# Mamba-2's z projected for two groups at once (512 columns, four PSUM banks) in groups 2 to 7

## The chip, the cores and the metric

One core of one Trainium2 chip runs the whole kernel in one launch. The metric is the device time of that launch in microseconds (us). The engines are named as in the profile: PE is the matrix engine (its weight loads are PEld), ACT the scalar engine, DVE the vector engine, POOL the general engine, SP the engine that issues DMAs.

## The reference, cut to what matters

Two layers over 512 tokens of width 1024, each a token mixer and a gated convolution. The first mixer is HGRN2, the second Mamba-2. The change is in Mamba-2, which has 8 groups of 4 heads:

```
def mamba2_mixer(u, w_in, ..., norm_w, w_out):
    z, xbc, dt_raw = jnp.split(u @ w_in, [D_INNER, D_INNER + CONV_DIM], axis=-1)
    xbc = jax.nn.silu(dwconv_centred(xbc, conv_w, conv_b))
    xs, bm, cm = jnp.split(xbc, [D_INNER, D_INNER + GN], axis=-1)
...
    y = (ssd_chunked(xs, dt_fw, a[0], bm, cm)
         + flip(ssd_chunked(flip(xs), flip(dt_bw), a[1], flip(bm), flip(cm)))
         + xs * d_skip.reshape(SSM_GROUPS, SSM_HPG, 1))
    y = y.reshape(bsz, seq, D_INNER) * jax.nn.silu(z)
    y = group_rmsnorm(y, norm_w, SSM_GROUPS)
    return y @ w_out
```

So z is a projection of u (512 tokens x 1024) to 2048 columns, 256 for each group. It is needed late in a group, where the group's y is multiplied by silu(z).

## The kernel before, in words

All projections are made of pairs of float32r values: every operand is split into a high and a low part, and a product is three matmuls (`mm3`, lines 164 to 166: high x high, low x high or high x low, and the other). A weight comes from HBM in pieces of 128 x 1024 floats through three `raw` buffers. ACT makes the high part of a piece (`whi`, line 138) and DVE the low one (`wlo`, line 139), four buffers each. The list `plan` fixes the order of the pieces, and `fetch` keeps two pieces ahead of the one in use.

Most projections hold a weight block still and stream u, 512 columns for a matmul (`proj_chs`). Only z (in Mamba) and one projection of HGRN2 are wanted with tokens on partitions: `proj_tok` holds a block of 128 tokens of u still and streams the 256 weight columns of one group. For z of one group that is 4 token blocks x 8 slices of the width x 3 = 96 matmuls of 256 columns, into two PSUM banks with two token blocks each.

PSUM has eight banks. `proj_ps` hands out three (`pp`), for projections and output projections, and `misc_ps` five (`pm`), for everything else. A bank is handed out again when the last instruction that reads it is done.

PE's order is written by hand. The string `MAMBA` (line 39) gives the order of the projections: `p` a group's B, C and x, `z` its z, `o` so many quarters of the output projection. `fill` issues them. Their length is counted in units, two units for six matmuls of 512 columns or for twelve of 256. The function `mix(g)` is the rest of group g, a generator whose nine steps are put into PE's stream at the units `STEPS` (33, 44, 45, 53, 56, 60, 64, 70, 89) after the start of the group's `p`, plus `LATE`. The order of ACT and DVE is not written by hand: the framework's scheduler decides it. The steps of `mix` that matter here, by their lines before:

- at 33: B is transposed into one `pm` bank (926) and B times C goes into another (931). ACT copies both out (927, 933).
- at 44: x is transposed into two `pm` banks (942), each copied out by ACT into `x_t` (943).
- at 53 and 56: the states of the two directions. Each takes two banks, `pa` with two products and `pb` with one (982). ACT copies the first product out (986), DVE makes the other two states by a multiply and an add each (991, 993), and only the adds read the bank.
- at 60 and 64: what the states give to the output, two banks each (1015), each read by one DVE multiply (1020).
- at 70: the products within a chunk into two banks (1030); DVE adds them and multiplies by silu(z) (1036, 1037). ACT squares, POOL makes the norm, ACT scales (1040 to 1045).
- at 89: y is transposed into two banks (1053). ACT writes its high part (`yh`, 1055) and DVE its low part (`yl`, 1056) from these banks. There are six `yh` and six `yl` buffers, so three groups' worth.

The output projection `out_part` takes groups in pairs: its quarters 0 to 3 read y of groups 0 and 1, 4 to 7 that of groups 2 and 3, 8 to 11 that of 4 and 5, and 12 to 15 that of group 6. A group's `yh` and `yl` buffers come free when the last quarter of its pair is done. Group 7 follows by itself.

Of the kernel before, what the change touches and what calls it, by code (L numbers as in the profile page):

```python
# [10 lines left out]
F32 = mybir.dt.float32  # L11
F32R = mybir.dt.float32r
I32 = mybir.dt.int32
U8 = mybir.dt.uint8
AF = mybir.ActivationFunctionType
# [4 lines left out]
P = 128  # L20
# [4 lines left out]
ND = D // P  # L25
# [10 lines left out]
LEVELS = (0, 5, 18, 32, 45)  # L36
ENDS = ((50, 55, 61, 67), (56, 61, 67, 74))

MAMBA = [(c[0], int(c[1:])) for c in "p0 z0 p1 z1 p2 z2 o1 p3 o1 z3 o2 p4 z4 o2 p5 z5 o2 p6 z6 p7 z7 o8".split()]

STEPS = (33, 44, 45, 53, 56, 60, 64, 70, 89)
LATE = {0: 21, 1: 1, 2: 4, 3: 4, 4: 2, 5: 3, 6: 3}
DTCOL = 64
SZ = 3

ARTANH = (0.11619523831039165, 0.1085165786592581, 0.14296291676788242, 0.19999850679099573, 0.33333333668798704)

# [12 lines left out]
def tile_trunk(ctx: ExitStack, tc: tile.TileContext, x, norm1_w, norm2_w, a_w_in, a_lb_logits, a_norm_w, a_w_out,  # L60
# [3 lines left out]
    V, A, G, PE = nc.vector, nc.scalar, nc.gpsimd, nc.tensor  # L64

    cst = ctx.enter_context(tc.tile_pool(name="cst", bufs=1))
    wp = ctx.enter_context(tc.tile_pool(name="wp", bufs=2))
    ps = ctx.enter_context(tc.tile_pool(name="ps", bufs=3, space=PSUM))
    dram = ctx.enter_context(tc.tile_pool(name="dram", bufs=1, space=DRAM))

    def proj_ps():
        return ps.tile([P, T], F32, tag="pp", name="pp", bufs=3)

    def misc_ps():
        return ps.tile([P, T], F32, tag="pm", name="pm", bufs=5)
# [12 lines left out]
    uhi = [cst.tile([P, T], F32R, name=f"uhi{d}") for d in range(ND)]  # L88
    ulo = [cst.tile([P, T], F32R, name=f"ulo{d}") for d in range(ND)]
    rbc = cst.tile([P, T], F32, name="rbc")  # L90
    ssum = cst.tile([P, T], F32, name="ssum")
    rtok = cst.tile([P, NB], F32, name="rtok")
# [20 lines left out]
    plan, ready = deque(), deque()  # L113

    def want(key, parts, nk):

        for k0 in range(0, nk, 4):
            plan.append((key, [x[k0 * P:min(nk, k0 + 4) * P] for x in parts]))

    def want_out(key, w_out, k0, nk):  # L120
        for c in range(4):
            want((key, c), [w_out[k0 * P:(k0 + nk) * P, c * 256:(c + 1) * 256]], nk)

    def load(parts):
        nk = parts[0].shape[0] // P
        raw = wp.tile([P, 4, 256], F32, tag="raw", name="raw", bufs=3)
        c0 = 0
        for src in parts:
            n = src.shape[1]
            nc.sync.dma_start(raw[:, :nk, c0:c0 + n], src.rearrange("(k p) c -> p k c", p=P))  # L130
            c0 += n
        return raw, nk, c0

    def halves(raw, nk, c0):
        hi = wp.tile([P, 4, 256], F32R, tag="whi", name="whi", bufs=4)
        lo = wp.tile([P, 4, 256], F32R, tag="wlo", name="wlo", bufs=4)
        r = raw[:, :nk, :c0]
        A.copy(hi[:, :nk, :c0], r)  # L138
        V.tensor_tensor(lo[:, :nk, :c0], r, hi[:, :nk, :c0].bitcast(F32), ALU.subtract)  # L139
        return hi, lo  # L140

    def fetch(n):
        while plan and len(ready) < n:
            k, parts = plan.popleft()
            ready.append((k, halves(*load(parts))))

    def take(key, ahead=2):

        got = []
        while (ready or plan) and (ready[0][0] if ready else plan[0][0]) == key:  # L150
            if not ready:
                k, parts = plan.popleft()
                ready.append((k, halves(*load(parts))))
            got.append(ready.popleft()[1])
        assert got, key
        fetch(ahead)

        def part(i, k, c0, n=P):
            return got[k // 4][i][:, k % 4, c0:c0 + n]

        return part

    def mm3(dst, lhi, llo, rhi, rlo, start, stop):
        PE.matmul(dst, lhi, rhi, start=start, stop=False)  # L164
        PE.matmul(dst, lhi, rlo, start=False, stop=False)  # L165
        PE.matmul(dst, llo, rhi, start=False, stop=stop)  # L166


    def proj_ch(p, w, c0):

        yield from proj_chs([(p, w, c0)])

    def proj_chs(ps):

        for k in range(ND):
            for p, w, c0 in ps:
                mm3(p, w(0, k, c0), w(1, k, c0), uhi[k], ulo[k], k == 0, k == ND - 1)
            if k % 2:
                yield 2 * len(ps)
# [97 lines left out]
    w_in = a_w_in[0]  # L277
# [16 lines left out]
    w_in = b_w_in[0]  # L294
    nout = 0
    for step in MAMBA:
        g = step[1]
        if step[0] == "p":
            want(("bc", g), [w_in[:, 4096 + P * g:4096 + P * (g + 1)], w_in[:, 5120 + P * g:5120 + P * (g + 1)]], ND)
            if g == 0:  # L300
                want("dt", [w_in[:, 6144:6208]] * 2, ND)
            want(("x", g), [w_in[:, 2048 + 256 * g:2048 + 256 * (g + 1)]], ND)
        elif step[0] == "z":
            want(("z", g), [w_in[:, 256 * g:256 * (g + 1)]], ND)
        else:
            for n in range(g):
                k, c = min(nout // 4 * 2, 6), nout % 4
                k1 = min(k + 2, 7)
                want((("bo", k), c), [b_w_out[0][2 * k * P:2 * k1 * P, c * 256:(c + 1) * 256]], 2 * (k1 - k))
                nout += 1  # L310
# [20 lines left out]
    parts = [plan.popleft()[1] for _ in range(4)]  # L331
# [94 lines left out]
    with tc.manual_schedule(engines={mybir.EngineType.PE, mybir.EngineType.DVE, mybir.EngineType.Activation}):  # L426
# [8 lines left out]
        w = halves(*raws[0])  # L435
# [12 lines left out]
        w = halves(*raws[2])  # L448
# [4 lines left out]
        w = halves(*raws[1])  # L453
# [4 lines left out]
        w = halves(*raws[3])  # L458
# [15 lines left out]
        w = take(("a", 0, 2))  # L474
# [305 lines left out]
    def mamba():  # L780
# [6 lines left out]
        def t2k(tag, bufs):  # L787
            return pool.tile([P, T], F32, tag=tag, name=tag, bufs=bufs)
# [25 lines left out]
        def r128(tag, bufs=2):  # L814
            return t2k(tag, bufs)[:, 0:H]

        def steps(x1):

            bias, na = dtbias, nega
            e, s, s2, acc = r128("sz", SZ), r128("th", 1), r128("pr"), r128("E1")  # L820
            V.tensor_scalar(x1, x1, bias, None, ALU.add)
# [42 lines left out]
            A.activation(fl(dec_t), fl(dec_t), AF.Exp)  # L864
            A.activation(fl(al_b), fl(al_b), AF.Exp)

        groups = {}

        def proj_group(g):
            wbc = take(("bc", g))  # L870
            r = []
            pbc, bc = [], ((16 + g, "sb", 1), (24 + g, "sc", 2))
            for i in range(2):
                pbc.append(proj_ps())
                if g == 0 and i == 0:
                    pd = proj_ps()
                    wd = take("dt")
                    yield from proj_chs([(pbc[0], wbc, 0), (pd, wd, 0)])
                else:
                    yield from proj_ch(pbc[i], wbc, i * P)  # L880
                if g > 0:
                    r.append(conv(pbc[i], i, *bc[i]))
            if g == 0:

                r.append(conv(pbc[0], 0, *bc[0]))
                x1 = r128("cb", 1)
                for n in range(2):
                    rs = slice(n * NR, (n + 1) * NR)
                    hs = slice(n * H, (n + 1) * H)
                    V.tensor_tensor(x1[rs], pd[rs, hs], rbc[rs, hs], ALU.mult)  # L890
                r.append(conv(pbc[1], 1, *bc[1]))
            wx = take(("x", g))
            for i in range(2):
                p = proj_ps()
                yield from proj_ch(p, wx, i * P)
                r.append(conv(p, i, 2 * g + i, "sx", 2))
                if g == 0 and i == 0:
                    step0 = steps(x1)
                    next(step0)
                    groups["steps"] = step0  # L900
            z = []
            groups[g] = (*r, z)

        def proj_z(g):
            z = groups[g][4]
            wz = take(("z", g))
            for c in range(2):
                p = proj_ps()
                yield from proj_tok(p, wz, (2 * c, 2 * c + 1))
                z.append(t2k("sz", SZ))  # L910
                for b in range(2):
                    bs = slice(b * 256, (b + 1) * 256)
                    A.activation(z[c][:, bs], p[:, bs], AF.Silu, scale=rtok[:, 2 * c + b:2 * c + b + 1])  # L913

        def h4(ap):

            return ap.rearrange("p n (h e) -> p n h e", e=64)
# [156 lines left out]
        def fill():  # L1074
            done = 0
            for kind, g in MAMBA:
                if kind == "p":
                    yield from proj_group(g)
                elif kind == "z":
                    yield from proj_z(g)  # L1080
                else:
                    done += g
                    while out_at[0] < out_units(done):
                        c = next(out_work)
                        out_at[0] += c
                        yield c
            yield from out_work

        def out_units(n):
            return 8 * min(n, 12) + 4 * max(n - 12, 0)  # L1090
# [8 lines left out]
        jobs, t, nout = [(scales(pool), [12, 18]), (step_columns(), [DTCOL])], 0, 0  # L1099
        for kind, g in MAMBA:  # L1100
            if kind == "p":
                if g == 0:
                    t += 8
                jobs.append((mix(g), [t + LATE.get(g, 0) + o for o in STEPS]))
                t += 32
            elif kind == "z":
                t += 16
            else:
                t += out_units(nout + g) - out_units(nout)
                nout += g  # L1110
# [112 lines left out]
```

## Time and profile before

| what | value |
|---|---|
| median of 3 runs | 1526.4 us (1526.35 to 1526.6) |
| time of the profiled execution | 1525.6 us |
| span of its instructions | 1523.8 us |
| PE busy | 1513.8 us, 99% of the span |
| DVE busy | 1040.2 us, 68% |
| ACT busy | 793.6 us, 52% |
| mean granted clock of PE | 0.999 |

The span is the time from the first to the last instruction. A launch is 1.8 us longer than it in the profiled execution. PE's busy time is the union of its matmuls, whose shown durations overlap their neighbours, so how long PE needs for a matmul is read from the distance of two starts, not from a duration.

### The profile page before, as it was taken

The page shows a single profiled execution, that of the slowest core. Times are in us where ns is not written, and L with a number is a line of the kernel's source. Part 1 is how long each engine was busy: PE and PEld are TensorE (multiplying, and loading weights), DVE is VectorE, ACT ScalarE, POOL GpSimd, SP SyncE. Part 2 cuts the span into 40 slices and gives each one's busy share as a digit, 9 for nine tenths or more (in the row PEclk, how much of TensorE's full clock was granted, in tenths as well). Part 3 has the DMA queues.
Part 4 walks back from the last instruction along what each step waited for, and adds up shares of the span by engine and source line. Part 5 has one row for each costly group of instructions (what it writes and reads, how often), then busy time and mean ns, then how long its engine had stood idle before and what let it go on. Part 6 is the DMA issues. An engine that isn't in the chain of part 4 may idle for free.

```text
span 1523.8 us, 24654 instructions
## 1 busy us (share of the span) xinstructions
PE 1513.8 (99%) x9935; PEld 1285.2 (84%) x9935; DVE 1040.2 (68%) x1695; ACT 793.6 (52%) x1427; POOL 29.3 (2%) x34
## 2 busy tenths in 40 slices
PE   9999999999999999999999999999999999999998
PEld 7888888888888888888888888888888888888887
DVE  6887786858564256545899978788878664346543
ACT  5656565545332133334699878569835433223333
POOL 0000000000000000000000000000000000000000
PEclk9999999999999999999999999999999999999999
DMA  5322222223333323223444343334223232323222
GB/s 186 111 76 67 70 72 64 70 77 111 97 97 97 97 97 98 90 90 109 129 138 138 124 124 116 108 114 128 66 79 122 86 110 84 97 97 111 76 83 77
DMA packets 153640, 151.65 MB, mean 100 GB/s; under 512 B 8390, under 2 KB 144279, under 8 KB 153527
## 3 DMA queue, kind: packets, MB, share of 16 engines
q1 hardware_dynamic: 153415, 149.93, 31.7%
q8 instruction: 78, 1.28, 0.4%
q14 instruction: 35, 0.29, 0.1%
q0 software_dynamic: 80, 0.15, 0.1%
q10 hardware_dynamic: 32, 0.01, 0.0%
HBM read 147.83 MB, written 2.23 MB: 98 GB/s over the span
## 4 chain that ended last, share of the span: by engine, by line
PE 89%; ACT 4%; DVE 3%; DMA 2%; issue 1%; POOL 0%; POOLq 0%; SPq 0%; DVEq 0%; ACTq 0%
PE pp L164 26%; PE pp L165 26%; PE pp L166 26%; PE pm L164 1%; PE pm L166 1%; PE pm L165 1%; ACT E L960 1%; PE pm L982 1%; PE pm L1015 1%; PE pm L677 1%; PE pm L568 1%; PE pm L1030 1%; PE pm L660 1%; DVE wlo L139 1%; DVE sx L810 1%
## 5 line engine op out<-in xcount | busy, mean ns | idle before, releaser
L164 PE MATMUL pp<-uhi,whi 128*128 128x512 f32 x1136 | 449.6, 396 | 1.2 <-ACT sz L913 0.9
L165 PE MATMUL pp<-ulo,whi 128*128 128x512 f32 x1136 | 442.5, 390 | 0.3 <-DVE ulo L212 0.3
L166 PE MATMUL pp<-uhi,wlo 128*128 128x512 f32 x1136 | 442.8, 390 | 0.0
L138 ACT CAST whi<-raw 128x1024 fp32r<-128x1024 f32 (+1 forms) x258 | 259.0, 1007 | 297.4 <-PE pp L165 229.1
L139 DVE TENSOR_TENSOR wlo<-raw,whi 128x1024 fp32r<-128x1024 f32 (+1 forms) x258 | 301.2, 1169 | 129.7 <-ACT whi L138 126.8
L164 PEld LDWEIGHTS pp<-uhi,whi 128*128 128x128 f32 x1136 | 213.3, 188 | 45.8 <-ACT sz L913 1.3
L166 PEld LDWEIGHTS pp<-uhi,wlo 128*128 128x128 f32 x1136 | 213.2, 188 | 45.3 <-DVE wlo L139 0.4
L165 PEld LDWEIGHTS pp<-ulo,whi 128*128 128x128 f32 x1136 | 213.4, 188 | 43.7 <-DVE ulo L212 0.9
L164 PE MATMUL pp<-yh,whi 128*128 128x512 f32 x460 | 182.8, 397 | 0.0
L166 PE MATMUL pp<-yh,wlo 128*128 128x512 f32 x460 | 179.3, 390 | 0.0
L165 PE MATMUL pp<-yl,whi 128*128 128x512 f32 x460 | 179.1, 389 | 0.0
L164 PE MATMUL pp<-whi,uhi 128*128 128x256 f32 x384 | 110.4, 287 | 0.0
L166 PE MATMUL pp<-whi,ulo 128*128 128x256 f32 x384 | 108.6, 283 | 0.0
L165 PE MATMUL pp<-wlo,uhi 128*128 128x256 f32 x384 | 108.6, 283 | 0.0
L272 DVE TENSOR_TENSOR h<-h,pp 128x512 f32<-128x512 f32 x80 | 54.2, 684 | 79.5 <-PE pp L166 79.0
L166 PEld LDWEIGHTS pp<-yh,wlo 128*128 128x128 f32 x460 | 86.3, 188 | 18.4
L164 PEld LDWEIGHTS pp<-yh,whi 128*128 128x128 f32 x460 | 86.4, 188 | 17.7 <-DVE h L272 0.3
L165 PEld LDWEIGHTS pp<-yl,whi 128*128 128x128 f32 x460 | 86.4, 188 | 17.4
L960 ACT ACTIVATE E<-R,col_t 128x128 f32<-128x128 f32 x256 | 81.7, 394 | 7.2 <-DVE E L964 4.9
L735 ACT ACTIVATE c<-gp,colp 128x512 f32<-128x512 f32 x44 | 35.7, 816 | 90.1 <-DVE gp L733 90.0
L737 DVE SCALAR_TENSOR_TENSOR c<-gp,colp,c 128x512 f32<-128x512 f32 x88 | 65.6, 750 | 19.2 <-ACT c L735 17.7
L164 PEld LDWEIGHTS pp<-whi,uhi 128*128 128x128 f32 x384 | 73.7, 192 | 0.6
(302 smaller groups left out, 2034.4 us busy)
## 6 DMA issues: line engine op xcount, KB each, us to landing
raw<-in_ffn_w_in_dram SPq DMA_DIRECT2D x88, 512.0 KB, 3.5
raw<-in_a_w_in_dram SPq DMA_DIRECT2D x40, 512.0 KB, 3.6
raw<-in_ffn_w_out_dram SPq DMA_DIRECT2D x40, 512.0 KB, 3.4
raw<-in_b_w_in_dram SPq DMA_DIRECT2D x32, 512.0 KB, 4.0
R<-ac_d SPq DMA_DIRECT2D x64, 256.0 KB, 3.7
raw<-in_b_w_in_dram SPq DMA_DIRECT2D x32, 256.0 KB, 4.0
raw<-in_b_w_out_dram SPq DMA_DIRECT2D x12, 512.0 KB, 3.4
xt<-in_x_dram SPq DMA_DIRECT2D x4, 512.0 KB, 8.5
```

Source lines behind the costliest of these rows:

```text
L138: A.copy(hi[:, :nk, :c0], r)
L139: V.tensor_tensor(lo[:, :nk, :c0], r, hi[:, :nk, :c0].bitcast(F32), ALU.subtract)
L164: PE.matmul(dst, lhi, rhi, start=start, stop=False)
L165: PE.matmul(dst, lhi, rlo, start=False, stop=False)
L166: PE.matmul(dst, llo, rhi, start=False, stop=stop)
L272: V.tensor_tensor(h[d], h[d], p, ALU.add)
L568: PE.matmul(p[j:j + Q, b * Q:(b + 1) * Q], lhs(b * P + j), rhs(b * P + j), start=True, stop=True)
L660: PE.matmul(pl[:, n * P:(n + 1) * P], kt[dr][:, n * P:(n + 1) * P], v[:, b, i * P:(i + 1) * P], start=True, stop=True)
L677: PE.matmul(po[:, ts], l, r, start=n == 0, stop=n == len(parts) - 1)
L735: A.activation(c, g[:, 0:T], AF.Identity, scale=col(W_FW[l], f), bias=col(W_FB, l * NFF + f))
L737: V.scalar_tensor_tensor(c, g[:, k:k + T], col(W_FW[l], k * NFF + f), c, ALU.mult, ALU.add)
L960: A.activation(e[:, bs], r[:, bs], AF.Identity, bias=col_t[:, b, dr * NH + hd:dr * NH + hd + 1])
```

## The change

In groups 2 to 7 z is projected for two groups in one go. The new fill element `w2` (and `w4`, `w6`) runs `proj_zs(g)`: it takes four banks at once, two `pp` and two `pm`, one for each token block, and streams 512 weight columns (both groups) past each held block of u. A weight piece is now 2 slices x 512 columns, not 4 x 256, so all four banks take their part of a piece before the next one is needed, and all four are open until the last piece. ACT then empties them, 256 columns at a time, into the z tiles of the two groups (`Z`). The z tiles get a fourth buffer (`SZ`). A `w` counts 32 units, as two `z` did. Groups 0 and 1 keep their own `z`. The string of the order changes:

```
-MAMBA = [... "p0 z0 p1 z1 p2 z2 o1 p3 o1 z3 o2 p4 z4 o2 p5 z5 o2 p6 z6 p7 z7 o8".split()]
+MAMBA = [... "p0 z0 p1 z1 p2 w2 o1 p3 o2 p4 w4 o1 p5 o2 p6 w6 p7 o10".split()]
-SZ = 3
+SZ = 4
...
-        for k0 in range(0, nk, 4):
-            plan.append((key, [x[k0 * P:min(nk, k0 + 4) * P] for x in parts]))
+        n = 4 if sum(x.shape[1] for x in parts) <= 256 else 2
+        for k0 in range(0, nk, n):
+            plan.append((key, [x[k0 * P:min(nk, k0 + n) * P] for x in parts]))
...
+    def next_piece(key):
+
+        if not ready:
+            fetch(1)
+        k, got = ready.popleft()
+        assert k == key, (k, key)
+        fetch(2)
+        return got
...
+        def proj_zs(g):
+
+            z = [Z.setdefault(g + i, []) for i in range(2)]
+            ps = [proj_ps(), proj_ps(), misc_ps(), misc_ps()]
+            for k0 in range(0, ND, 2):
+                w = next_piece(("z", g))
+                for b, p in enumerate(ps):
+                    bs = slice(b * P, b * P + P)
+                    for k in (k0, k0 + 1):
+                        mm3(p, uhi[k][:, bs], ulo[k][:, bs], w[0][:, k - k0, :], w[1][:, k - k0, :],
+                            k == 0, k == ND - 1)
+                    yield 2
+            for b, p in enumerate(ps):
+                for i in range(2):
+                    if b % 2 == 0:
+                        z[i].append(t2k("sz", SZ))
+                    A.activation(z[i][b // 2][:, b % 2 * 256:b % 2 * 256 + 256], p[:, i * 256:(i + 1) * 256], AF.Silu,
+                                 scale=rtok[:, b:b + 1])
```

In the changed file the lines are shifted: 942 became 972, 943 973, 960 990, 963 993, 982 1012, 986 1016, 1053 1083, 1055 1085, 811 823, 138 141.

How the order moved, at the three places that matter. A row gives the line, the operation, out<-in, the size, and which engines' semaphores the instruction waits for.

PE, the states of group 4 (step 53). Before, they stand in an output projection:

```order
L982 MATMUL pm_9395<-xd_9352,bt_9249 128x256 [waits DVE_49,PE_49]
L982 MATMUL pm_9395<-xd_9352,bt_9249 128x256
L982 MATMUL pm_9396<-xd_9352,bt_9249 128x256 [waits PE_49]
```

Now they stand inside `w4`, and the transposes of group 3's y (1083) and of group 4's x (972) stand shortly ahead of them, also inside `w4` (its own two `pm` banks are 9066 and 9067):

```order
L1083 MATMUL pm_9147<-ident_66,y_8858 128x128 [waits Activation_49]
L1083 MATMUL pm_9147<-ident_66,y_8858 128x128 x3
L972 MATMUL pm_9155<-ident_66,sx_8974 128x128 [waits Activation_49]
...
L972 MATMUL pm_9161<-ident_66,sx_8974 128x128 [waits Activation_49]
...
L1012 MATMUL pm_9208<-xd_9173,bt_9086 128x256 [waits DVE_49]
L1012 MATMUL pm_9208<-xd_9173,bt_9086 128x256
L1012 MATMUL pm_9209<-xd_9173,bt_9086 128x256 [waits DVE_49,Activation_49]
```

The first write into `pb` (9396 before, 9209 now) waited for PE alone; now it waits for DVE and ACT, which read `pa` (9208).

ACT, in the same stretch, behind the copies of group 4's transposed B and of B times C, up to the first copy of its x. Before:

```order
L960 ACTIVATE E1_9485<-R_9483,col_t_6785 128x128
...
L960 ACTIVATE E1_9978<-R_9976,col_t_6785 128x128 [waits DMAHW3_49,DVE_49]
L138 CAST whi_9363<-raw_9360 128x1024 [waits DMAHW7_49,DMAHW6_49,PE_49]
L943 COPY xt_9327<-pm_9328 128x512 [waits PE_49]
L943 COPY xt_9327<-pm_9334 128x512 [waits PE_49]
```

Now (a table load for line 993 stands ahead of the first row):

```order
L993 ACTIVATE E1_9268<-E1_9268 128x512 [waits DVE_49]
L990 ACTIVATE E0_9289<-R_9287,col_t_6785 128x128
L141 CAST whi_9179<-raw_9177 128x1024 [waits DMAHW1_49,PE_49]
L823 ACT_TABLE_LOAD
L823 ACTIVATE sx_9057<-sx_9057 128x512 [waits DVE_49]
L990 ACTIVATE E1_9296<-R_9294,col_t_6785 128x128 [waits DMAHW5_49]
L990 ACTIVATE E1_9296<-R_9294,col_t_6785 128x128 x3
L990 ACTIVATE E0_9306<-R_9304,col_t_6785 128x128 [waits DMAHW7_49]
L990 ACTIVATE E0_9306<-R_9304,col_t_6785 128x128 x2
L993 ACT_TABLE_LOAD
L993 ACTIVATE E1_9296<-E1_9296 128x512 [waits DVE_49]
L973 COPY xt_9154<-pm_9155 128x512 [waits PE_49]
```

The two copies of x stood next to each other; now three rows of line 990 stand between the first and the second.

ACT, the writes of group 5's y. Before, they stand ahead of the copy of group 6's B (10379):

```order
L1055 ACTIVATE yh_10302<-pm_10304,colp_102 128x512 [waits PE_49]
L1055 ACTIVATE yh_10311<-pm_10313,colp_102 128x512 [waits PE_49]
L138 CAST whi_10343<-raw_10340 128x1024 [waits DMAHW5_49,DMAHW4_49]
...
L927 COPY bt_10379<-pm_10380 128x512 [waits PE_49]
```

Now group 5's (10130, 10139) stand with group 6's (10560, 10569) behind the copies of group 7's x:

```order
L973 COPY xt_10664<-pm_10665 128x512 [waits PE_49]
L993 ACTIVATE E1_10822<-E1_10822 128x512 [waits DVE_49]
L973 COPY xt_10664<-pm_10671 128x512 [waits PE_49]
L1085 ACTIVATE yh_10128<-pm_10130,colp_102 128x512 [waits PE_49]
L1085 ACTIVATE yh_10137<-pm_10139,colp_102 128x512 [waits PE_49]
L1085 ACTIVATE yh_10558<-pm_10560,colp_102 128x512 [waits PE_49]
L141 CAST whi_10833<-raw_10831 128x1024 [waits DMAHW0_49,PE_49]
L1085 ACTIVATE yh_10567<-pm_10569,colp_102 128x512 [waits PE_49]
```

So group 5's y stays in its two `pm` banks over a whole group more than before.

## Rows read from the trace of the kernel before

**Rows 1.** The page: the span, and PE's busy time.

```profile
span 1523.8 us, 24654 instructions
PE 1513.8 (99%) x9935; PEld 1285.2 (84%) x9935; DVE 1040.2 (68%) x1695; ACT 793.6 (52%) x1427; POOL 29.3 (2%) x34
```

**Rows 2.** PE's waits from 690 to 1160 us: total, times, longest.

```profile
PE pp L164 <- ACT sz L913: 0.9, 1, 0.9
```

**Rows 3.** Busy time by stretch; the first row's 1.00 is the granted clock.

```profile
950.00:1005.00 55.00, 55.00 (x359) 48.10 (x358) 42.10 (x73) 37.09 (x79) 1.95 (x1) 1.00 0.36 109
...
sum 215.00, PE 215.00 PEld 187.97 DVE 176.19 ACT 159.75 POOL 5.88; mean PE 53.75 PEld 46.99 DVE 44.05 ACT 39.94 POOL 1.47
```

**Rows 4.** PE's timeline around z of group 0: start, duration.

```profile
719.32 0.39 PE L164 MATMUL pp<-uhi,whi 128*128 128x512 f32 x1
...
732.24 0.28 PE L164 MATMUL pp<-whi,uhi 128*128 128x256 f32 x1
...
743.76 0.40 PE L164 MATMUL pp<-uhi,whi 128*128 128x512 f32 x1
```

**Rows 5.** PE's timeline: quarters 3 and 7 end, y of groups 3, 5.

```profile
906.96 0.39 PE L166 MATMUL pp<-yh,wlo 128*128 128x512 f32 x1
...
924.39 0.38 PE L1053 MATMUL pm<-ident,y 128*128 128x128 f32 x2
...
1014.18 0.39 PE L166 MATMUL pp<-yh,wlo 128*128 128x512 f32 x1
...
1038.33 0.27 PE L1053 MATMUL pm<-ident,y 128*128 128x128 f32 x1
```

**Rows 6.** Timeline, group 4's step at 33: PE, and ACT's copy.

```profile
934.96 0.27 PE L926 MATMUL pm<-ident,sb 128*128 128x128 f32 x1
935.40 1.06 PE L931 MATMUL pm<-sc,sb 128*128 128x128 f32 x8
936.21 0.36 PE L164 MATMUL pp<-whi,uhi 128*128 128x256 f32 x1
...
935.60 0.59 ACT L927 COPY bt<-pm 128x512 f32<-128x512 f32 x1 [0.60 <-PE pm L926]
```

**Rows 7.** Groups by line, 890 to 1105 us: busy us, mean ns.

```profile
L960 ACT ACTIVATE E<-R,col_t 128x128 f32<-128x128 f32 x122 | 39.6, 396 | 6.3 <-DVE E L964 4.4 <-PE pm L1030 1.8
L138 ACT CAST whi<-raw 128x1024 fp32r<-128x1024 f32 x31 | 32.2, 1045 | 6.8 <-PE pp L165 6.7
L963 ACT ACT_TABLE_LOAD x11 | 14.1, 1283 | 10.7 <-DVE E L962 10.6
L963 ACT ACTIVATE E<-E 128x512 f32<-128x512 f32 x15 | 9.5, 630 | 0.1
L913 ACT ACTIVATE sz<-pp,rtok 128x256 f32<-128x256 f32 x18 | 7.7, 469 | 0.1
```

**Rows 8.** Timeline, group 7's x: PE's transposes, ACT's first copy.

```profile
1095.88 0.27 PE L942 MATMUL pm<-ident,sx 128*128 128x128 f32 x1
...
1099.37 0.58 ACT L943 COPY xt<-pm 128x512 f32<-128x512 f32 x1
```

**Rows 9.** Timeline, states: group 4's (PE, DVE), and an ACT copy of group 7.

```profile
951.27 0.38 PE L982 MATMUL pm<-xd,bt 128*128 128x256 f32 x1
...
954.96 0.43 DVE L991 TENSOR_TENSOR hin<-hin,al_b 128x256 f32<-128x256 f32 x1 [0.98 <-ACT hin L986]
955.50 0.42 DVE L993 TENSOR_TENSOR hin<-hin,pm 128x256 f32<-128x256 f32 x1
...
1106.06 0.35 ACT L986 COPY hin<-pm 128x256 f32<-128x256 f32 x1
```

**Rows 10.** Timeline, group 7's step at 60: PE, and the reading DVE row.

```profile
1110.69 0.38 PE L1015 MATMUL pm<-hin,sc 128*128 128x256 f32 x1
...
1112.28 0.42 DVE L1020 TENSOR_TENSOR pr<-pm,ec_t 128x256 f32<-128x256 f32 x1
```

More of the change, by code (lines that the diff above doesn't have):

```diff
@@ L37 @@
 ENDS = ((50, 55, 61, 67), (56, 61, 67, 74))
-MAMBA = [(c[0], int(c[1:])) for c in "p0 z0 p1 z1 p2 z2 o1 p3 o1 z3 o2 p4 z4 o2 p5 z5 o2 p6 z6 p7 z7 o8".split()]
+MAMBA = [(c[0], int(c[1:])) for c in "p0 z0 p1 z1 p2 w2 o1 p3 o2 p4 w4 o1 p5 o2 p6 w6 p7 o10".split()]
 STEPS = (33, 44, 45, 53, 56, 60, 64, 70, 89)
@@ L124, in load @@
     def load(parts):
-        nk = parts[0].shape[0] // P
-        raw = wp.tile([P, 4, 256], F32, tag="raw", name="raw", bufs=3)
+        nk, c = parts[0].shape[0] // P, sum(x.shape[1] for x in parts)
+        raw = wp.tile([P, 2, 512] if c > 256 else [P, 4, 256], F32, tag="raw", name="raw", bufs=3)
         c0 = 0
@@ L134, in halves @@
     def halves(raw, nk, c0):
-        hi = wp.tile([P, 4, 256], F32R, tag="whi", name="whi", bufs=4)
-        lo = wp.tile([P, 4, 256], F32R, tag="wlo", name="wlo", bufs=4)
+        shape = [P, 2, 512] if c0 > 256 else [P, 4, 256]
+        hi = wp.tile(shape, F32R, tag="whi", name="whi", bufs=4)
+        lo = wp.tile(shape, F32R, tag="wlo", name="wlo", bufs=4)
         r = raw[:, :nk, :c0]
@@ L302, in tile_trunk @@
             want(("x", g), [w_in[:, 2048 + 256 * g:2048 + 256 * (g + 1)]], ND)
-        elif step[0] == "z":
-            want(("z", g), [w_in[:, 256 * g:256 * (g + 1)]], ND)
+        elif step[0] in "zw":
+            want(("z", g), [w_in[:, 256 * g:256 * (g + (1 if step[0] == "z" else 2))]], ND)
         else:
@@ L865, in steps @@
             A.activation(fl(al_b), fl(al_b), AF.Exp)
-        groups = {}
+        groups, Z = {}, {}
         def proj_group(g):
@@ L900, in proj_group @@
                     groups["steps"] = step0
-            z = []
-            groups[g] = (*r, z)
+            groups[g] = (*r, Z.setdefault(g, []))
         def proj_z(g):
@@ L1080, in fill @@
                     yield from proj_z(g)
+                elif kind == "w":
+                    yield from proj_zs(g)
                 else:
@@ L1105, in mamba @@
                 t += 32
-            elif kind == "z":
-                t += 16
+            elif kind in "zw":
+                t += 16 if kind == "z" else 32
             else:
```

## The prediction

> **What bounds the kernel now.** I read the page first, then PE's waits, then the stretch around the change, then the timeline. PE is busy for 1513.8 of 1523.8 us [rows 1]. Over the whole of Mamba and its edges (690 to 1160 us) the list of waits has one line for PE, a single wait of 0.9 us for the emptying of a z bank [rows 2]. So each us that PE needs less, or waits more, is a us of the kernel. From 890 to 1105 us, PE is busy all 215 us at a granted clock of 1.00, while DVE is busy for 176.2 (82%) and ACT for 159.8 (74%) [rows 3]. These two have some air, but they answer late: they serve a queue, and nobody at PE waits for them, since five `pm` banks are enough for all of it.
>
> **What it removes.** In groups 2 to 7, 6 x 96 = 576 matmuls of 256 columns become 288 of 512. By durations (0.28 and 0.39) this would be 161 - 112 = 49 us, but durations overlap. From 719.32 to 732.24 us there are 57 starts of 512 columns, 0.2267 us each; from 732.24 to 743.76 there are 96 of 256 columns, 0.1200 us each [rows 4]. Two of 256 take 0.2400, so a pair saves 0.0133 us, and 288 pairs **3.8 us**. That is all the gain there is.
>
> The Trainium skill (TensorE: Matmul & The Clock Gate, Back-to-back issue gap) gives N / 2.4 ns plus about 2.5 ns for each matmul. By it the halved count would save 288 x 2.5 ns = 0.7 us; the trace's 13 ns each is five times that, and the row decides. Nothing below uses the page's figure.
>
> **What costs nothing.** The weights are as many bytes and pieces as before, and a piece still feeds 24 matmuls of 512 (5.4 us) where ACT's cast takes 1.04 [rows 7]; the fetching stays two pieces ahead. The z banks are emptied by as many ACT rows. A unit is 3 x 0.2267 = 0.68 us. z comes later in the first group of a pair (unit 64 behind its `p`, where it was 48); its eight rows take 8 x 0.47 = 3.8 us [rows 7], and DVE wants it at step 70, 8 to 10 units or 5.4 to 6.8 us behind the `w`. If they slipped past that, step 89 would be late next, 19 units or 13 us further on. The fourth z buffer lets a `w` take all four: the last users, of the group before, are done some 40 units earlier.
>
> **What it costs: `pm` banks.** Two things take them. First, each `w` holds two of five for its 32 units (some 22 us plus the steps inside), and the steps 33 to 60 of its first group fall into it. Second, the order of the quarters has moved against the six `yh` buffers. Before, quarter 3 ended at 907 us, ahead of group 3's transposes at 924, and quarter 7 at 1014, ahead of group 5's at 1038 [rows 5]. Now quarter 3 stands behind `w4` (group 3's transposes are at unit 93 from its `p`, quarter 3 ends at 120), and quarter 7 behind `p7` (group 5's: 92 against 160). Groups 3 and 5, and group 6 behind them (140 against 160, counted from group 5's `p`), find all `yh` buffers taken, so their transposed y waits in its two banks. The order shows ACT's rows for groups 5 and 6 behind the copies of group 7's x. So in `w4` and `w6` from the transposes on, 5 - 2 - 2 = **one** `pm` bank is left, and around the start of `o10`, 5 - 2 - 2 = one again. Each step that takes two banks then makes PE wait for the reading of the first before it writes the second. PE's queue is in order, so the matmuls of the `w` behind it wait too.
>
> Which waits: the second x bank in `w4`, `w6` and `o10` (3 times, X); `pb` in both directions in `w4` and `w6`, and in the second direction in `w2`, where three banks are left (5 times, H); the second bank of step 60 in `w4` and `w6`, which waits for its neighbour or for the first emptied z bank (twice, P); B times C behind B's copy in `o10` (once, B).
>
> The trace of before holds no such wait. Its bounds are these. The floor is an answer at once. B's copy began 0.64 us behind its first transpose and ended 1.23 behind it, and four transposes take 0.44 [rows 6]: 0.8 us of wait, for X and B. For H: a product 0.38, copy 0.35, multiply 0.43, add 0.42 and three handovers of 0.1 make 1.9, less PE's two products 0.76: 1.1. For P: one DVE row of 0.42 and handovers, 0.6. Floors together: 4 x 0.8 + 5 x 1.1 + 2 x 0.6 = 9.9 us. The upper bound is the lag that the same rows had when nobody waited. Group 7's x: 1095.88 to 1099.95, less 0.44: 3.6 [rows 8]. Group 4's states: 951.27 to 955.92, less 0.76: 3.9 [rows 9]. Step 60: 1110.69 to 1112.70, less 0.38: 1.6 [rows 10]. Together 4 x 3.6 + 5 x 3.9 + 2 x 1.6 = 37.1 us.
>
> Between them I go by the new order. A row of line 960 takes 39.6 / 122 = 0.325 us, a cast 1.04, a load 1.28, an exponential 0.63 (the silu taken alike) [rows 7]. In `w4`, from the first transpose of B: ACT begins at 0.64, then two copies 1.18, a load, an exponential, one 960, a cast, a load, the silu, seven 960, a load, an exponential and the copy of x: 11.8 us. PE meanwhile has 1.25 for B and C [rows 6], 30 matmuls (6.8) and 12 transposes (1.3): 9.4. Wait X = 2.4. In `w6` ACT's list is the same and PE has 36 matmuls: X = 1.0. From the copy of x to the states' copy ACT has 13 rows of 960, the other copy, two casts, two exponentials and the copy in `w4` (8.5 us, with DVE 9.4) against PE's 0.44 + 6.8 + 0.76 = 8.0: H = 1.4. In `w6` 13 of 960, two casts, one exponential, two copies (7.9, with DVE 8.8) against 24 matmuls, 6.6: H = 2.2. The second direction: `w4` 4 of 960, a load, one z row, the copy (3.4, with DVE 4.35) against 3.45: 0.9; `w6` likewise 1.1. `w2` at the floor, 1.1. P by halves, 1.0 each; X in `o10` 2.0 and B 1.5, nearer to the floor, since ACT has only just copied there. Sum: 5.4 + 6.7 + 2.0 + 1.5 = 15.6 us. This takes ACT as never waiting itself. In rows 7 its 960 rows and loads sat idle for 17.0 of 215 us, 8%; on lists of some 50 us that is 4, of which I take 3. **18.6 us of waits, less 3.8: 14.8 us.** The sum stands against the profiled 1525.6 us, 0.8 below the median; I put it on the median: **1541 us**, 1% slower.
>
> **Rivals.**
> *The banks come back in time* (faster). If group 3's and 5's y found buffers after all, or the copies came within PE's own 0.44 and 0.76 us, nothing would wait, and 3.8 us are left: 1522.6. It decides at a lag below 0.8 us; the shortest that the rows show for a copy is 1.23, and the new order has ACT's `yh` rows late. 4%.
> *The waits and the gain cancel* (same): 1 to 7 us of waits, 1523.5 to 1529.5. It needs fewer waits than I count, as when the two z banks of a `w` come free for step 53 already. They don't: all four are open to the last piece. 7%.
> *ACT and DVE answer as late as they do now* (much slower): 26 to 40 us of waits, 1549 to 1562. For it: the new order still puts a dozen rows ahead of the first copy. Against it: while PE waits, they work off their queue, and DVE's rows for the states stand together. 20%.
> *The clock falls.* Every stretch of Mamba shows 1.00 [rows 3], with no long wait in it, so no row shows what a series of waits of 1 to 3 us does. If the 15 us behind the first wait in `w4` and in `w6` ran at 1.2 GHz, twice 15 us would be added: 1571. The Trainium skill (TensorE: Matmul & The Clock Gate, A second HAM failure mode: psum-queue depth-cycling) tells of a kernel that cycled through PSUM banks, whose small gaps made the clock swing; no run here shows it so far. 4%.
>
> **How the numbers follow.** The likeliest, 10 to 26 us of waits, has 63% and the range 1532 to 1549; 2% are left for what I don't see. Slower by over 0.2% (3.1 us, about what a measurement of this kernel can tell from no change): 63 + 20 + 4 + 1 = 88%; same 7%; faster 5%. The range for 8 in 10 runs from just under the floors (1530) to just under the upper bound (1557).
>
> **What would show it.** Right: 512-column starts 0.227 us apart in the `w`s; PE waits on ACT at 972 and on DVE or ACT at 1012, some eleven of 0.6 to 4 us, most of them in `w4` and `w6`, 12 to 24 us in total; the copies 973 apart from each other; group 5's `yh` behind quarter 7. Wrong: no PE waits at 972 and 1012; or PE waiting for weights or z; or a granted clock below 1 in Mamba; or a gain in the `w`s far from 3.8 us.

## The result, and the profile after

The changed kernel takes 1547.02 us (median of 4 runs, 1546.34 to 1548.2), the kernel before on the same chip 1526.5 (4 runs): a ratio of 1.0135, 95% interval 1.0123 to 1.0148. That is slower by 20.5 us; 1541 had been forecast, 14.8 slower. The profiled execution took 1546.34 us. Its page, beside [rows 1]:

```profile
span 1544.6 us, 24083 instructions
...
PE 1515.6 (98%) x9647; PEld 1271.4 (82%) x9647; DVE 1043.8 (68%) x1695; ACT 783.3 (51%) x1417; POOL 27.8 (2%) x34
```

There are 288 matmuls fewer, yet PE is busy 1.8 us longer, and 19 us of idle time have come in. They are all in Mamba. PE's waits from 690 to 1200 us (total, times, longest), where [rows 2] had one line:

```profile
PE pm L1012 <- DVE hin L1023: 8.1, 4, 2.5
PE pm L972 <- ACT xt L973: 5.9, 3, 2.9
PE pm L961 <- ACT bt L957: 2.3, 1, 2.3
PE pm L1012 <- ACT sz L942: 2.1, 1, 2.1
PE pm L1045 <- ACT sz L942: 0.5, 1, 0.5
PE pp L176 <- DVE xp L818: 0.4, 1, 0.4
PE pm L1060 <- DVE E L994: 0.2, 1, 0.2
```

Line 972 is x's transposes, 1012 the states, 961 B times C, 1045 the step at 60 (in before 942, 982, 931 and 1015), 1060 the step at 70. PE's timeline has each wait in brackets behind the row that waited (the waits of 0.2 and 0.4 us, at 813 and 823 us, are left out):

```profile
848.32 0.67 PE L1012 MATMUL pm<-xd,bt 128*128 128x256 f32 x2 [2.15 <-ACT sz L942]
942.34 0.66 PE L972 MATMUL pm<-ident,sx 128*128 128x128 f32 x4 [2.90 <-ACT xt L973]
954.76 0.67 PE L1012 MATMUL pm<-xd,bt 128*128 128x256 f32 x2 [2.48 <-DVE hin L1023]
959.22 0.67 PE L1012 MATMUL pm<-xd,bt 128*128 128x256 f32 x2 [1.54 <-DVE hin L1023]
963.59 1.13 PE L1045 MATMUL pm<-hin,sc 128*128 128x256 f32 x4 [0.50 <-ACT sz L942]
1055.89 0.66 PE L972 MATMUL pm<-ident,sx 128*128 128x128 f32 x4 [1.99 <-ACT xt L973]
1065.43 0.70 PE L1012 MATMUL pm<-xd,bt 128*128 128x256 f32 x2 [2.52 <-DVE hin L1023]
1072.84 0.67 PE L1012 MATMUL pm<-xd,bt 128*128 128x256 f32 x2 [1.54 <-DVE hin L1023]
1107.90 1.16 PE L961 MATMUL pm<-sc,sb 128*128 128x128 f32 x8 [2.30 <-ACT bt L957]
1117.39 0.66 PE L972 MATMUL pm<-ident,sx 128*128 128x128 f32 x4 [1.06 <-ACT xt L973]
```

The first stands in `w2`, the next four in `w4` or just behind, three in `w6` or just behind, the last two at the start of `o10`. The first is put down to `sz`, but the `sz` rows that end there read `pp` banks, and the state wants a `pm` bank. DVE's add of the first direction (1023), which reads a `pm` bank, ends at 848.17, 0.15 us ahead of the start, so this is most likely a wait for the states' own bank, as in `w4`.

Why a bank is short in `w4` is read from the y of group 3, which [rows 5] had ready at 924.39. Its transposes on PE (x8 is both halves, so two banks), a matmul of quarter 3, and ACT's rows that empty those two banks:

```profile
937.96 1.03 PE L1083 MATMUL pm<-ident,y 128*128 128x128 f32 x8
...
970.44 0.39 PE L178 MATMUL pp<-yh,wlo 128*128 128x512 f32 x1
...
970.87 1.37 ACT L1085 ACTIVATE yh<-pm,colp 128x512 fp32r<-128x512 f32 x2 [2.95 <-PE pp L178]
```

The two banks stay taken for 33 us, since ACT's row waits for that matmul, a reader of the `yh` that is to be overwritten; ACT stands idle for 2.95 us before it. For group 5 the same takes from 1049.66 to 1118.77 us.

The longest wait, from both sides. ACT's timeline in `w4`, from B's copy to the copy of x:

```profile
931.66 0.56 ACT L957 COPY bt<-pm 128x512 f32<-128x512 f32 x1
932.13 0.58 ACT L963 COPY cb<-pm 128x512 f32<-128x512 f32 x1
932.72 1.28 ACT L993 ACT_TABLE_LOAD   x1
934.02 0.63 ACT L993 ACTIVATE E<-E 128x512 f32<-128x512 f32 x1
934.55 0.39 ACT L990 ACTIVATE E<-R,col_t 128x128 f32<-128x128 f32 x1
934.85 1.03 ACT L141 CAST whi<-raw 128x1024 fp32r<-128x1024 f32 x1
935.90 1.28 ACT L823 ACT_TABLE_LOAD   x1
937.19 0.64 ACT L823 ACTIVATE sx<-sx 128x512 f32<-128x512 f32 x1
937.73 2.14 ACT L990 ACTIVATE E<-R,col_t 128x128 f32<-128x128 f32 x7
939.89 1.28 ACT L993 ACT_TABLE_LOAD   x1
941.18 0.63 ACT L993 ACTIVATE E<-E 128x512 f32<-128x512 f32 x1
941.72 0.57 ACT L973 COPY xt<-pm 128x512 f32<-128x512 f32 x1
```

It is the list that the prediction added up, row for row, and ACT has no gap in it. PE in the same stretch:

```profile
936.60 0.39 PE L176 MATMUL pm<-whi,uhi 128*128 128x512 f32 x1
...
937.74 0.39 PE L178 MATMUL pm<-whi,ulo 128*128 128x512 f32 x1
...
938.84 0.60 PE L972 MATMUL pm<-ident,sx 128*128 128x128 f32 x4
...
943.07 0.63 PE L177 MATMUL pm<-wlo,uhi 128*128 128x512 f32 x1
...
946.48 0.40 PE L176 MATMUL pp<-whi,uhi 128*128 128x512 f32 x1
946.71 0.39 PE L177 MATMUL pp<-wlo,uhi 128*128 128x512 f32 x1
```

From 936.60 to 937.74 there are five steps of 0.228 us: the matmuls of 512 columns start as [rows 4] had them. x's second bank then waits 2.90 us. But from 943.07 to 946.48 eight steps of the same matmuls take 0.426 us each, and the next one 0.23 again. Busy time by stretch, with the granted clock behind POOL's share:

```profile
938.00:941.00 3.00, 1.44 (x13) 1.20 (x11) 0.96 (x3) 2.98 (x8) 0.00 (x0) 1.00 0.67 193
941.00:943.00 2.00, 0.66 (x5) 0.66 (x6) 0.69 (x1) 1.99 (x6) 0.00 (x0) 1.00 0.27 103
943.00:946.50 3.50, 3.50 (x10) 2.68 (x10) 2.83 (x3) 2.60 (x7) 0.00 (x0) 0.51 0.39 138
946.50:949.50 3.00, 3.00 (x15) 2.48 (x14) 2.85 (x5) 2.78 (x9) 0.00 (x0) 1.00 0.29 79
```

Behind the wait PE runs at a granted clock of 0.51, which is the lower level, 1.2 GHz, for 3.4 us, half of which is lost: 1.7 us. The same happens once more from 1065.9 to 1069.3 us, behind the wait of 2.52: together 3.4 us.

**The account.** From 690 to 1200 us PE is idle 510 - 490.24 = 19.8 us, and 0.9 before: 18.9 more. With 3.4 for the clock this is 22.3; the span has grown by 20.8. So all else has saved 1.5 us, not 3.8.

### The profile page after: what moved, and what is told of

It reads as the page before. It is cut to its first block, busy times and chain, and to the rows that moved or that the text cites. A ratio compares the mean times of both kernels' runs of the same rounds, so it can differ in the third digit from the quotient of the medians.

```text
span 1544.6 us, 24083 instructions
## 1 busy us (share of the span) xinstructions
PE 1515.6 (98%) x9647; PEld 1271.4 (82%) x9647; DVE 1043.8 (68%) x1695; ACT 783.3 (51%) x1417; POOL 27.8 (2%) x34
## 4 chain that ended last, share of the span: by engine, by line
PE 81%; DVE 9%; ACT 6%; issue 2%; DMA 1%; POOL 1%; POOLq 0%; DVEq 0%; SPq 0%; ACTq 0%
PE pp L176 23%; PE pp L177 23%; PE pp L178 23%; DVE wlo L142 2%; PE pm L176 2%; PE pm L178 2%; PE pm L177 2%; ACT E L990 1%; DVE sx L822 1%; PE pm L689 1%; PE pm L580 1%; ACT whi L141 1%; PE pm L1045 1%; ACT L993 1%; PE pm L1012 1%
## 5 line engine op out<-in xcount | busy, mean ns | idle before, releaser
L749 DVE SCALAR_TENSOR_TENSOR c<-gp,colp,c 128x512 f32<-128x512 f32 x88 | 65.6, 750 | 18.9 <-ACT c L747 17.5
L176 PE MATMUL pp<-whi,uhi 128*128 128x256 f32 (+1 forms) x240 | 76.2, 317 | 0.4 <-DVE xp L818 0.4
L177 PE MATMUL pp<-wlo,uhi 128*128 128x256 f32 (+1 forms) x240 | 73.9, 308 | 0.0
L178 PE MATMUL pp<-whi,ulo 128*128 128x256 f32 (+1 forms) x240 | 73.8, 307 | 0.0
L745 DVE TENSOR_TENSOR gp<-pp,rbc 128x512 f32<-128x512 f32 x40 | 27.7, 693 | 50.7 <-PE pp L178 50.2
```

The costliest lines, as they stand in the source:

```text
L745: V.tensor_tensor(g[:, 1:T + 1], p, rbc, ALU.mult)
L749: V.scalar_tensor_tensor(c, g[:, k:k + T], col(W_FW[l], k * NFF + f), c, ALU.mult, ALU.add)
```

## The experiments

Beside each measured time stand three numbers of its profiled execution against that of before, worked out as above: PE's idle time in Mamba, the clock's loss while PE was busy, and what is left of the span's difference (rest). Runs of the kernel before range over 2 us (1525.19 to 1527.14 in one set), so a rest is good to about 1 us. In the rows, `xp` is a projection's result as DVE takes it out of its bank, `sx` is x before it is transposed, and `xd` is the transposed x times its decay.

**1. Which of the two takers?** The forecast names two: the banks that a `w` holds, and the late y that holds two more. Three kernels take away the one, the other, or both. In the first, the ring holds eight (the edit is cut to the arguments that change; `th` and `R` make room).

```
-name="yh", bufs=6   -name="yl", bufs=6   -t2k("th", 1)   -t2k("R", 4)
+name="yh", bufs=8   +name="yl", bufs=8   +t2k("pr", 2)   +t2k("R", 3)
```

> The changed kernel with eight yh and eight yl buffers in place of six, so that y of groups 3 and 5 finds buffers in time (group 6's stays 20 units late); to make room, th shares the buffers of pr and R has three buffers. Theory (two takers: each w's two pm banks and the late y's two together leave one): w4 and w6 then have three pm banks, as w2 has now, where one wait of 2.1 us stands. Waits 6 to 10 us (some 2 in each w, up to 3.4 at o10), no fall of the clock, less the 3.8 of the pairs: 1529 to 1533 us. Rival (the w's two banks alone make the waits): the waits of w4 and w6 stay, 1543 to 1548. Rival (two z at once put ACT and DVE behind, whatever the banks): also 1541 to 1548.

Measured: 1529.41 us, ratio 1.0021 (1.0011 to 1.003), as the theory said; idle 5.5, clock 0, rest -1.2. The longest of PE's waits in Mamba, and ACT's row for group 3's y, whose transposes begin at 939.87:

```profile
PE pm L1012 <- DVE hin L1023: 1.6, 1, 1.6
PE pm L1012 <- ACT sz L942: 1.5, 1, 1.5
PE pm L972 <- DVE yl L1086: 1.2, 1, 1.2
```

```profile
941.00 0.67 ACT L1085 ACTIVATE yh<-pm,colp 128x512 fp32r<-128x512 f32 x1
```

ACT takes up y 1.1 us behind its first transpose, where that took 33.

17.6 of the 20.5 us are gone with two more buffers, all waits at 972 and 1012 in `w6` and `o10` among them. The next kernel keeps six buffers, and writes each `w` as two z (`z2 z3` for `w2`, and so on; `proj_z` then takes its tiles from `Z`):

> The changed kernel's order of the work with each w written as two z (256 columns, one bank at a time from the pp banks), six yh buffers: y of groups 3, 5 and 6 is as late as in the changed kernel, but no z takes a pm bank. Theory (two takers): three pm banks are left where one was, so waits of 1 to 2 us in three places at most, 1527 to 1533 us. Rival (the w's banks alone): no wait at all, 1526 to 1527.5. Rival (the late y alone): most of the 19.5 us stay, 1540 to 1548.

Measured: 1532.07 us, 1.0035 (1.0023 to 1.0048); idle 4.1, clock 1.7, rest +1.0. This is in the theory's range, but the fall of the clock was not in it. Three waits: B's 2.3 us at `o10` with the fall behind it, 1.1 for x, 1.1 for the states. With neither taker:

> As the run with two z for each w, and with eight yh and yl buffers (th in pr's buffers, three R): neither taker is there but for group 6's y. Theory: no wait over 1 us, the time of the kernel before, 1526 to 1527.5, since the 3.8 us of the pairs are not there either. Rival (the order of the work puts ACT and DVE behind): 1530 to 1545.

Measured: 1529.35 us, 1.002 (1.001 to 1.0029); idle 1.7, clock 0, rest +1.3. It missed its range by 2 us: waits of 1.0 and 0.8 at 1045 and 1083, and a rest of 1.3, which this order and these buffers cost without the `w`. By idle time and clock, less the 1.7 of this run, late y alone costs 4.1 us (4.1 + 1.7 - 1.7), the `w`'s banks alone 3.8 (5.5 - 1.7), and both together 20.6 (18.9 + 3.4 - 1.7): neither single rival holds. The pairs' gain, by the rests at the same buffers: -1.2 against +1.3, and -1.5 (the changed kernel) against +1.0: **2.5 us**, good to some 1 us.

**2. The other remedy: quarters in time.** Six buffers, and the quarters moved ahead of the y that needs their buffers; `w` for groups 2 to 5 alone.

```
-p0 z0 p1 z1 p2 w2 o1 p3 o2 p4 w4 o1 p5 o2 p6 w6 p7 o10
+p0 z0 p1 z1 p2 w2 o1 p3 o3 p4 w4 p5 o4 p6 z6 p7 z7 o8
```

> Six yh buffers, z for two groups at once in groups 2 to 5 alone, and the quarters moved so that every y finds a buffer: p0 z0 p1 z1 p2 w2 o1 p3 o3 p4 w4 p5 o4 p6 z6 p7 z7 o8. Theory (two takers): w2 and w4 with three pm banks, a wait of some 2 us each, less two thirds of 3.8 us: 1526 to 1530 us. Rival (the w's banks alone): the five waits of w2 and w4 stay, some 9 us and a fall of the clock of 1.7, less 2.5: 1534 to 1536.

Measured: 1528.98 us, 1.0018 (1.0008 to 1.0027); idle 3.2, clock 1.7, rest -1.7. A wait of 2.2 in `w2`, one of 1.1 in `w4`: as the theory said, but for the fall of the clock behind the first. Then the states' steps are put behind the `w` as well:

```
-LATE = {0: 21, 1: 1, 2: 4, 3: 4, 4: 2, 5: 3, 6: 3}
+LATE = {0: 21, 1: 1, 2: 12, 3: 4, 4: 12, 5: 3, 6: 3}
```

> The kernel of w24_early with the steps of groups 2 and 4 at LATE 12, six yh buffers. Theory (banks): the 2.2 us wait in w2, the 1.1 us one in w4 and the 1.7 us of lowered clock behind the first go, 1523.5 to 1526 us. Rival (ACT is behind there whatever the banks): the waits come back at the states' steps, 1527 to 1531.

Measured: **1524.41 us**, 0.9987 (0.9977 to 0.9996), against 1526.34 for the kernel before: faster than that and than the changed kernel. Its ten runs (1523.63 to 1524.71) all lie below the 18 of the kernel before beside them (1525.37 to 1526.79). All of PE's waits from 690 to 1200 us that are left:

```profile
PE pp L176 <- DVE xp L818: 0.4, 1, 0.4
PE pm L1060 <- DVE E L994: 0.2, 1, 0.2
```

Its control has the same order and steps, with z in place of `w`:

> The kernel of w24_early_late12 with w2 and w4 written as z2 z3 and z4 z5: the same order of all else, the same steps, 256 columns. Theory (the 1.9 us by which w24_early_late12 is below the kernel before are 192 pairs x 0.0133 us = 2.6, less some 0.7 for the order): no wait, 1526.4 to 1527.4 us. Rival (the order and the later steps bring it, the pairs nothing): 1524 to 1525.

Measured: 1525.81 us, 0.9996 (0.9988 to 1.0005); idle -0.6, clock 0, rest 0.0, where `w24_early_late12` has -0.1, 0 and -1.5. It lies between the theory and its rival: the 192 pairs bring 1.4 us by the medians, 1.0 by the profiled spans, 1.5 by the rests, not 2.6. The two sets of runs do not overlap; they are of two chips, on which the kernel before took 1526.34 and 1526.32. PE's own rows agree: from start to next start, the 768 z matmuls take 93.3 us, and 91.7 when 384 of them are 192 pairs. Of the 91.7 us, 0.4 are the wait for `xp` above, so that the pairs themselves bring 2.0 by this count.

**3. Fewer `pm` banks for a `w`.**

```
-ps = [proj_ps(), proj_ps(), misc_ps(), misc_ps()]
+ps = [proj_ps(), proj_ps(), proj_ps(), misc_ps()]
```

> The changed kernel with each w on three pp banks and one pm bank in place of two and two; six yh buffers, so y is late as in the changed kernel. Theory (two takers): two pm banks are left in w4 and w6 where one was, four in w2; the waits for x's second bank (some 5 us) go, those for the states' pb shrink; a wait of up to 1.5 us for the emptied pp bank behind each w comes new: 8 to 14 us of waits, 1532 to 1540 us. Rival (ACT late, whatever the banks): 1544 to 1550.

Measured: 1530.55 us, 1.0027 (1.0018 to 1.0037); idle 5.6, clock 3.4, rest -2.6. Below the expected range: with two banks left where one was, x in `w4` and `w6` never waits, two waits for the states are left (2.7; the waits for B and x at `o10`, 2.3 and 1.1, stay), and the wait for an emptied `pp` bank didn't come. So one bank more is worth some 16 us: the price is steep in the last bank.

**4. Later steps, without more buffers or another order.**

```
-LATE = {0: 21, 1: 1, 2: 4, 3: 4, 4: 2, 5: 3, 6: 3}
+LATE = {0: 21, 1: 1, 2: 21, 3: 4, 4: 21, 5: 3, 6: 21}
```

> The changed kernel with one line altered: LATE 21 for groups 2, 4 and 6, so that of the steps of a w's first group only B and B times C fall into the w, and group 6's y comes two units ahead of quarter 7's end; order and buffers as in the changed kernel. Theory (two takers meet the steps of two banks): B's copy is waited for in w4 and w6 (two waits of 1 to 2 us), x and the states find three banks or more: waits of 2 to 5 us, 1525 to 1530 us. Rival (the late y's alone, or ACT being late, make the waits, wherever the steps stand): 1536 to 1547.

Measured: 1532.96 us, 1.0045 (1.0031 to 1.0058), between the theory and its rival; idle 6.4, clock 2.8, rest -2.4. B's two waits came, 3.4 us in all as the theory had them, and no state waits; but a wait of 3.3 us for group 7's x (for ACT's silu of `sx`) is new, with the clock down from within that wait on. Moving a step is not free. That ACT was late there because it then met the next group's work is argued, not shown. The same shows in the next, 8 buffers and later steps:

> The kernel of w_ring8 with the steps of groups 2 and 4 eight and ten units later and of group 6 twenty later (LATE 12, 12, 23), so that the states' steps of a w's first group stand behind the w, and group 6's y behind quarter 7. Theory (banks): with neither taker at the steps that need two banks, no wait over 1 us is left in Mamba, and the gain of the pairs shows: some 4 to 5 us below w_ring8, 1523 to 1526 us. Rival (the gain of 3.8 us is not there at all): 1526.5 to 1529.

Measured: 1531.96 us, 1.0038 (1.0023 to 1.0052), 2.5 us above `w_ring8` where 4 to 5 below was expected: idle 6.8, clock 1.7, rest -1.7. The states' waits are gone, and two waits for `sx` (3.4 us) have come. This theory asked only where banks are free, and not when x is. And once more, a `w` for groups 0 and 1:

> The kernel of w24_early_late12 with a w for groups 0 and 1 too: p0 w0 p1 p2 w2 p3 o4 p4 w4 p5 o4 p6 z6 p7 z7 o8, 288 pairs in all. Theory (the pairs' gain is there wherever no step of two banks falls on two taken ones): 96 x 0.0133 = 1.3 us below w24_early_late12, 1522.8 to 1524 us. Rival (step_columns, which takes three banks at unit 64 inside w0, waits for copies, and group 1's later steps fall into w2): 1525 to 1529.

Measured: 1538.99 us, 1.0079 (1.0066 to 1.0093). The rival was right in its sign, but 10 us too low, and not right in its cause: no wait falls in `w0`. Group 0's states, in `p1`, wait 3.6 us for `xd`, since ACT empties the four banks of `w0` ahead of its copies of x; group 1's x, now in `p2` with no `z1` before it, waits 6.1 us for `sx`:

```profile
PE pm L972 <- ACT sx L823: 6.1, 1, 6.1
PE pm L1012 <- DVE xd L1002: 3.6, 1, 3.6
```

**5. Does a wait lower the clock?** Eight waits are put into the last FFN (the gated convolution) of the kernel before, behind a pair of gates, with n = 2, 4, 6, 8, 6, 8, 10, 14 (cut to the helper; PE's order in that FFN is fixed by hand as well).

```
+pt = misc_ps()
+PE.transpose(pt[:, 0:P], ident, ident)
+wt = pool.tile([P, P], F32, tag="wt", name="wt", bufs=2)
+A.copy(wt, pt[:, 0:P])
+for _ in range(n):
+    A.copy(wt, wt)
+po = misc_ps()
+PE.transpose(po[:, 0:P], wt, ident)
```

> The kernel before with eight waits put into the last FFN on purpose, where PE is busy throughout: behind each gate pair a transpose, a copy and a chain of 2, 4, 6, 8, 6, 8, 10 and 14 more copies of 128x128 on ACT, and a second transpose that waits for them (the result is the kernel before's). Theory (a wait of over 2 us can be followed by 3.4 us at the lower clock, a shorter one is not): no fall behind the first two waits, falls of 3.4 us behind some or all of the longer. Rival (the falls in the changed kernel had another cause than PE's wait): none here. Time: the sum of the waits and 1.7 us for each fall, some 1545 to 1560 us.

Measured: 1573.77 us (one run), above the range. The waits came out longer than aimed at, 2.20, 2.85, 3.51, 4.55, 3.56, 4.56, 5.21 and 6.53 us, so no short one was tried. The stretches of the first, behind it, and behind the second (the granted clock stands ahead of the last two numbers):

```profile
1184.00:1189.00 5.00, 2.80 (x14) 2.06 (x13) 4.75 (x7) 3.20 (x7) 0.00 (x0) 1.00 0.33 105
1189.00:1193.00 4.00, 4.00 (x12) 3.17 (x11) 1.34 (x2) 0.63 (x1) 0.00 (x0) 0.57 0.44 131
1215.00:1235.00 20.00, 19.99 (x89) 16.58 (x90) 8.62 (x11) 5.48 (x7) 0.00 (x0) 1.00 0.26 79
```

Behind the wait of 2.20 the clock fell for 3.4 us, behind that of 2.85 it did not, nor behind 3.56; behind the other five it fell for 3.4 to 6.8 us, from within the wait on. Up to the end of the launch the clock falls nowhere else in this kernel. So a wait of PE is enough for a fall, though not each time, and the rival is out. Idle 33.0 us and 12.1 of clock are 45.1 of the 48.2 that the span grew.

## Why the prediction was right, and what it missed

The sign, the place and the cause are as forecast; 20.5 us is within the range, 6 us above the point. Two of the prediction's own signs of being wrong came all the same, a granted clock below 1 in Mamba and a gain far from 3.8 us; they make up the 6 us.

**The waits.** Forecast and measured, in us: x in `w4` 2.4 and 2.90, in `w6` 1.0 and 1.99, at `o10` 2.0 and 1.06; states in `w2` 1.1 and 2.15, in `w4` 1.4 + 0.9 and 2.48 + 1.54, in `w6` 2.2 + 1.1 and 2.52 + 1.54; the step at 60 in `w4` and `w6` 2.0 and 0.50; B at `o10` 1.5 and 2.30. The sum was 15.6, and 3 for ACT's own waits made 18.6; measured 18.9 more idle time than before. The states were undersized (6.7 against 10.2), by about what the allowance of 3 held, and the step at 60 oversized: that the totals meet within 0.3 is in part luck. [rows 6 to 9] gave bounds; the order of ACT's rows gave the size. What the sum had not counted for the states shows in `w4`: a low-part row of DVE's (142) stands between ACT's copy and the states' multiply (1021), so that the add (1023) ends 1.85 us behind the copy, where the sum had 0.9. In `w6` it is the same.

```profile
952.41 0.36 ACT L1016 COPY hin<-pm 128x256 f32<-128x256 f32 x1
952.53 1.22 DVE L142 TENSOR_TENSOR wlo<-raw,whi 128x1024 fp32r<-128x1024 f32 x1 [2.62 <-ACT whi L141]
953.67 0.42 DVE L1021 TENSOR_TENSOR hin<-hin,al_b 128x256 f32<-128x256 f32 x1
954.20 0.42 DVE L1023 TENSOR_TENSOR hin<-hin,pm 128x256 f32<-128x256 f32 x1
```

**The two takers.** Shown: late y alone leaves 4.1 us of idle time, the `w`'s banks alone 5.5, both together 18.9, and y's banks are seen to stand 33 and 69 us. That ACT's row waits for a quarter is in its own line above. The rival that ACT and DVE answer late whatever the banks is out for `w4` and `w6`: with the ring of eight, much the same ACT rows stand ahead of x's copy in `w4`, and x waits 1.2 us there and not at all in `w6`.

**The gain** is the term that was mis-sized: 288 pairs x 0.0133 gave 3.8; by the rests it is 2.5, and 1.0 to 2.0 for two thirds of it. The spacing of undisturbed starts was right: in `w_ring8`, z's 512-column starts lie 0.2267 us apart from the twelfth in a row on. But the steps of `mix` break up the z, and behind a break the second to the eleventh start are followed by the next after 0.2299 us on average (160 starts, 0.5 us in all). Those of 256 columns, in `z_ring8`, are followed after 0.1193 there, no later than elsewhere. The remaining 0.8 us is not settled.

**The clock** is the term that was missing. It stood as a rival of 4% with two stretches of 15 us; in truth two waits in ten were followed by 3.4 us at 1.2 GHz each, a loss of 3.4 us in sum. The Trainium skill (TensorE: Matmul & The Clock Gate, A second HAM failure mode: psum-queue depth-cycling) tells of frequent small idle gaps, in a kernel that cycles through PSUM banks, that make the clock swing. The traces here agree that idle time at PSUM banks can bring the clock down, but show it at single waits of 1.9 us and more alone.

So 18.9 + 3.4 - 1.5 = 20.8 on the profiled spans, where 18.6 - 3.8 had been put; that 1.5 is the pairs' 2.5 less some 1.0 that the new order costs without any `w`.

## What to carry to other kernels

Before an operation is given more banks at once, count who else holds banks at that moment, above all results that wait for a buffer which a later piece of work must first set free: two modest takers that met cost five times here what each cost alone. A merge of matmuls saves no more than the spacing of their starts, here 13 ns a pair at best, so one wait of 2 us eats 150 pairs; the version that won merged fewer, moved the freeing work forward, and kept the steps that want two banks out of the merged stretch. When steps are moved, ask where their inputs then come from, not only which banks are free.

## What the hardware showed that was not expected

A single wait of PE can cost more than its length: behind waits of 1.9 to 2.9 us the granted clock fell to 1.2 GHz for 3.4 us, a loss of 1.7 us, and at most of the longer ones for 3.4 to 6.8 us, from within the wait on. It is not a fixed price: in the changed kernel waits of 2.15, 2.48 and 2.30 us were followed by none, and in the kernel with the added waits those of 2.85 and 3.56 were not either. In none of the kernels did the clock fall in Mamba behind waits under 1.9 us alone. What decides between two waits of like length stays open.
